# Local attention on one core: the two heads of a pair alternate on halves of TensorE's array (values by columns, scores by rows)

## The chip, the cores and the metric

The kernel runs on one core of a Trainium2 chip. The metric is the device time of one execution in microseconds; the time of a kernel is the median of several runs. TensorE multiplies 128x128 tiles, ScalarE (ACT) and VectorE (DVE) take the results out of PSUM (8 banks of 128 x 512 float32) and prepare operands, GpSimd (POOL) does small things, and SyncE (SP) issues the transfers.

## What is computed

One decoder block on 512 tokens with 1024 features, all in float32: a retention mixer with 4 heads and a sliding-window attention with 8 query heads and 2 key heads run side by side on the same normed input, are gated and merged, and a squared-ReLU MLP follows. The change touches the sliding-window attention only. Of the reference, that is:

```python
SWA_HEADS, SWA_KV_HEADS, SWA_DH, WINDOW = 8, 2, 64, 128
# q: (1, 512, 8, 64); k, v: (1, 512, 2, 64); blocks of 128 tokens
# kk, vv: the previous block and the block itself, 256 keys for each block of queries
s = jnp.einsum('bnigrd,bnjgd->bgrnij', qb, kk).astype(f32) * (dh ** -0.5)
s = s - slopes * dist                       # a slope for each head
s = jnp.where(blk_valid, s, -jnp.inf)       # 0 <= dist < 128; block 0 has no previous block
m = jnp.maximum(jnp.max(s, axis=-1, keepdims=True), sink)
p = jnp.exp(s - m)
p = p / (jnp.sum(p, axis=-1, keepdims=True) + jnp.exp(sink - m))
out = jnp.einsum('bgrnij,bnjgd->bnigrd', p, vv.astype(f32))
```

Around it: `x += RMSNorm((sigmoid(gate_r) * y_r + sigmoid(gate_s) * y_s) @ W_out)`, where `y_s` is this output times `W_swa_out`, and then the MLP.

## The kernel before

Most products are made in three passes of the type float32r: each operand is split into a rounded part (`split`, L124, ACT) and the remainder (L125, DVE), and `mm3` (L167 to L169) multiplies hi by hi, hi by lo and lo by hi. Some small products are made with plain float32 operands instead: the scores of the retention (`ret_scores`, L534), the values of the attention (L506, L510). A plain float32 product leaves two matmul records, and two weight loads, for each call in the trace; a float32r product leaves one.

The attention stage is a loop over 4 steps `h` (L626). Step `h` treats one retention head and one pair of attention heads (2h and 2h+1, which share a key head). In a step TensorE runs, in this order: the scores of the pair (`swa_scores`), the projection of the retention's queries (`project_copy` to `qT`), the transposes of the step before (`ret_out`), the projection of the keys (`kT`), the transposes of the attention's probabilities (`swa_transpose`, L488, L490), those of the keys (`ret_keys`), the next step's retention values (`project_v`), the retention's scores (`ret_scores`), the attention's values (`swa_values`), the retention's states (`ret_states`, tile `ret_st`), two gate projections with the next pair's queries between them (`swa_queries`, L662), and the retention's values (`ret_values`, tile `ret_v`). A planner in the framework sets the order on each engine from the order of the program, priorities and modelled times; `issue_after` holds instructions back behind a named one. All PSUM tiles come from one pool of 8 banks.

Queries of a pair come out of one projection as 128 rows, 64 for each head. `swa_queries` makes for each head `g` a tile `qs2[g]` of 128 rows: the rounded part on the head's own 64 rows (ACT, L419) and the remainder on the other 64 (DVE, L420). The keys `ksT` hold the 64 key rows twice, in a rounded part and a remainder (L623, by `split`). So a score product contracts over 128 rows with a stacked split, and two products (`part`, L446 to L451) over 256 key columns make a block: 16 matmuls of 128x256 for the pair. In step 0 the queries first go through a copy `rg` that multiplies by the norm factors `R` (L389), since that projection is made from the input that is not yet normed.

`swa_values` (L498) multiplies the transposed probabilities with the 64 value columns of the key head. Head 0 writes rows 0 to 63 of one bank `pso`, head 1 rows 64 to 127; all seven products of head 0 come first (one of L506 and one of L510 for each block but block 0), then the seven of head 1. The result is split to `swaT` (L513).

Of the kernel before, what the change touches and what calls it, by code (L numbers as in the profile page):

```python
# [10 lines left out]
F32 = mybir.dt.float32  # L11
F32R = mybir.dt.float32r
AF = mybir.ActivationFunctionType
ALU = mybir.AluOpType
PSUM = bass.MemoryType.PSUM

P = 128
D_MODEL = 1024
SEQ = 512
NT = SEQ // P  # L20
# [67 lines left out]
def f(ap):  # L88
    return ap.bitcast(F32)
# [3 lines left out]
def block_kernel(ctx, tc, x, xT, pre_mix, w_in, w_gate, w_ret, w_swa, w_out, sinks, post_mix,  # L93
# [10 lines left out]
    def bank(shape, name="ps"):  # L104
        return psum.tile(shape, F32, tag="ps", name=name)
# [279 lines left out]
    def project_copy(dst, w, first):  # L385

        ps = project_block(w, xg if first else hT)
        if first:
            nc.vector.tensor_tensor(dst, ps, R, op=ALU.mult)  # L389
        else:  # L390
            nc.scalar.copy(dst, ps)
# [15 lines left out]

    def swa_queries(w, first=False):

        if first:  # L410
            ps = rpool.tile([P, SEQ], F32, name="rg", bufs=2)
            project_copy(ps, w, True)
        else:
            ps = project_block(w)
        rows = [slice(g * SWA_DH, (g + 1) * SWA_DH) for g in range(2)]
        qs2 = []
        for g in range(2):
            q2 = dpool.tile([P, SEQ], F32R, name=f"qs2{g}", bufs=1)
            q_hi = nc.scalar.mul(q2[rows[g]], ps[rows[g]], SWA_DH**-0.5)  # L419
            q_lo = nc.vector.scalar_tensor_tensor(  # L420
                q2[rows[1 - g]], ps[rows[g]], SWA_DH**-0.5, f(q2[rows[g]]),
                op0=ALU.mult, op1=ALU.subtract,
            )
            qs2.append(q2)
        return (qs2, (q_hi, q_lo)) if first else qs2

    def swa_scores(b, qs2):
        bias = dpool.tile([P, 2, 2 * P], F32, name="bias", bufs=1)
        m = asmall.tile([P, 2, NT], F32, name="m")
        den = asmall.tile([P, 2, NT], F32, name="den")  # L430
        sexp = asmall.tile([P, 2, NT], F32, name="sexp")
        negm = asmall.tile([P, 2, NT], F32, name="negm")
        probs = []
        for g in range(2):
            head = 2 * b + g
            nc.vector.tensor_scalar(
                bias[:, g, :], dist_sb, float(2.0 ** (-8.0 / SWA_HEADS * (head + 1))), None,
                op0=ALU.mult,
            )
            s = dpool.tile([P, NT, 2 * P], F32, name="s", tag="s")  # L440
            for bp in range(2):
                ps = bank([P, 2, 2 * P], "swa_s")
                for i in range(2):
                    blk = 2 * bp + i
                    k0 = max(blk - 1, 0) * P
                    for part in range(2):  # L446
                        nc.tensor.matmul(
                            ps[:, i, :], qs2[g][:, blk * P : (blk + 1) * P],
                            ksT[part][:, b // 2, k0 : k0 + 2 * P],
                            start=part == 0, stop=part == 1,  # L450
                        )  # L451
                for i in range(2):
                    blk = 2 * bp + i
                    lo = P if blk == 0 else 0
                    nc.vector.tensor_tensor_reduce(
                        s[:, blk, lo:], ps[:, i, : 2 * P - lo], bias[:, g, lo:], 1.0,
                        sink_sb[:, head : head + 1], ALU.add, ALU.max,
                        accum_out=m[:, g, blk : blk + 1],
                    )
            nc.vector.tensor_scalar(negm[:, g, :], m[:, g, :], -1.0, None, op0=ALU.mult)  # L460
            nc.vector.tensor_scalar(
                sexp[:, g, :], m[:, g, :], -1.0, sink_sb[:, head : head + 1],
                op0=ALU.mult, op1=ALU.add,
            )
            for blk in range(NT):
                lo = P if blk == 0 else 0
                nc.scalar.activation(
                    s[:, blk, lo:], s[:, blk, lo:], AF.Exp, bias=negm[:, g, blk : blk + 1],
                    accum_out=den[:, g, blk : blk + 1],
                )  # L470
            nc.scalar.activation(sexp[:, g, :], sexp[:, g, :], AF.Exp)
            nc.vector.tensor_add(den[:, g, :], den[:, g, :], sexp[:, g, :])
            nc.vector.reciprocal(den[:, g, :], den[:, g, :])
            for blk in range(NT):
                lo = P if blk == 0 else 0
                nc.vector.tensor_scalar(
                    s[:, blk, lo:], s[:, blk, lo:], den[:, g, blk : blk + 1], None, op0=ALU.mult
                )
            probs.append(s)
        return probs  # L480
# [17 lines left out]
    def swa_values(b, probs_t):  # L498
        pso = bank([P, SEQ], "pso")
        c0 = P + (b // 2) * SWA_DH  # L500
        for g, (pd, pp) in enumerate(probs_t):
            rows = slice(g * SWA_DH, (g + 1) * SWA_DH)
            for blk in range(NT):
                o = pso[rows, blk * P : (blk + 1) * P]
                if blk:
                    nc.tensor.matmul(  # L506
                        o, kv[:, blk - 1, c0 : c0 + SWA_DH], pp[:, blk - 1, :],
                        start=True, stop=False,
                    )
                nc.tensor.matmul(  # L510
                    o, kv[:, blk, c0 : c0 + SWA_DH], pd[:, blk, :], start=blk == 0, stop=True
                )
        split(swaT[0][:, b, :], swaT[1][:, b, :], pso)  # L513

# [94 lines left out]

    pending = None  # L610
    q = load_queries(0)
    qs2, qs_last = swa_queries(q[0], True)
    kk2 = dpool.tile([P, SWA_KV, NT, 2, SWA_DH], F32, name="kk2", tag="s")
    ksT = [dpool.tile([P, SWA_KV, SEQ], F32R, name=f"ksT{i}", bufs=1) for i in range(2)]
    for g in range(SWA_KV):
        for i in range(2):
            nc.gpsimd.tensor_copy(kk2[:, g, :, i, :], kv[:, :, g * SWA_DH : (g + 1) * SWA_DH])
        ps = bank([P, SEQ])
        for t in range(NT):
            nc.tensor.transpose(  # L620
                ps[:, t * P : (t + 1) * P], kk2[:, g, t].rearrange("p i d -> p (i d)"), ident
            )
        split(ksT[0][:, g, :], ksT[1][:, g, :], ps)  # L623
    v0_block(3)
    v0_out(3)
    for h in range(RET_HEADS):  # L626
        probs = swa_scores(h, qs2)
        qT = dpool.tile([P, SEQ], F32, name="qT", bufs=1)
        project_copy(qT, q[1], h == 0)
        qc = [dpool.tile([P, SEQ - P], F32R, name=f"qc{i}", bufs=1) for i in range(2)]  # L630
        split(qc[0], qc[1], qT[:, P:])
        if pending is not None:
            ret_out(*pending)
        kr = load_feature_blocks(w_in, (C_KR + h * RET_DK,))
        kT = dpool.tile([P, SEQ], F32, name="kT", bufs=1)
        project_copy(kT, kr[0], h == 0)
        if h == 0:
            with ExitStack() as order:
                for ins in qs_last:
                    order.enter_context(tc.issue_after(ins.ins))  # L640
                for k in range(KD):
                    norm_input(k)
            uctx0.close()
            actx = ExitStack()
            apool = actx.enter_context(tc.tile_pool(name="apool", bufs=1, side="right"))
            retT = [apool.tile([P, KD, SEQ], F32R, name=f"retT{i}") for i in range(2)]
            swaT = [apool.tile([P, 4, SEQ], F32R, name=f"swaT{i}") for i in range(2)]
        probs_t = swa_transpose(probs)
        kd = ret_keys(kT, h)
        v = v_next  # L650
        if h + 1 < RET_HEADS:
            v_next = project_v(h + 1)
        pt = ret_scores(qT, kT, h)
        swa_values(h, probs_t)
        states = ret_states(kd, v, h)
        g = load_feature_pair(w_in, C_GR + h * RET_DV)
        silu = rpool.tile([P, 2, SEQ], F32, name="silu")
        if h + 1 < RET_HEADS:
            q = load_queries(h + 1)
        for e in range(2):  # L660
            if e == QS_AT and h + 1 < RET_HEADS:
                qs2 = swa_queries(q[0])  # L662
            ps = project_block(g[e])
            nc.scalar.activation(silu[:, e, :], ps, AF.Sigmoid)
            nc.vector.tensor_tensor(silu[:, e, :], ps, silu[:, e, :], op=ALU.mult)
        retn = ret_values(qc, pt, states, v, h)
        pending = (retn, silu, h)
# [537 lines left out]
```

## Time and profile before

| | us |
|---|---|
| median of 3 runs | 753.0 (752.38 to 754.23) |
| the profiled execution | 751.75 |
| its span in the profile | 750.0 |
| TensorE busy in the span | 738.2 (98%) |
| VectorE busy | 545.6 (73%) |
| ScalarE busy | 400.1 (53%) |

The profiled execution is 1.75 us longer than its span, and 1.25 us shorter than the median. In the trace a matmul record starts when the array takes it and its end is modelled, so the records of a run of matmuls overlap: the distance from start to start is what one costs. Where a row stands for several instructions (x8), its first number is the first start and its second the time to the last end; the start of the last one is that end less the duration of a single one. PEld is the loading of the stationary operand, which has a row of its own.

### The profile page before, as it was taken

What the parts mean: (1) busy time and instruction counts of PE and PEld (TensorE: products, weight loads), DVE (VectorE), ACT (ScalarE), POOL (GpSimd) and SP (SyncE); (2) the same over time, 40 slices, a digit from 0 to 9 for tenths busy, and PEclk for the clock granted to TensorE, in tenths of its full rate; (3) what the DMA queues carried; (4) which work ended last, traced back from release to release, by engine and by line L of the source; (5) the groups of instructions that cost most, each with busy time, mean ns of one, the idle gap of its engine ahead of it and who ended that gap; (6) DMA issues with size and microseconds to landing.
All of it is one profiled execution on the core that took longest, in us unless ns stands there. A gap on an engine that the chain in (4) does not pass through costs nothing.

```text
span 750.0 us, 11710 instructions
## 1 busy us (share of the span) xinstructions
PE 738.2 (98%) x4678; PEld 668.5 (89%) x4678; DVE 545.6 (73%) x847; ACT 400.1 (53%) x642; POOL 50.1 (7%) x67
## 2 busy tenths in 40 slices
PE   8999999999999999999999999999999999999996
PEld 8979899898888989899888999999999888888885
DVE  5695474655868867776755787688779778986796
ACT  6683464354554544343542775566556655655571
POOL 0200000000001000000001200000000011010010
PEclk9999999999999999999999999999999999999999
DMA  8614312312015584553483326876763899789503
GB/s 298 202 56 142 97 44 59 111 29 85 29 57 155 144 241 122 141 146 100 147 324 113 94 62 218 205 195 170 185 169 113 292 296 206 173 180 214 112 1 112
DMA packets 51863, 109.42 MB, mean 146 GB/s; under 512 B 3425, under 2 KB 31457, under 8 KB 47713
## 3 DMA queue, kind: packets, MB, share of 16 engines
q1 hardware_dynamic: 46480, 80.89, 32.3%
q0 software_dynamic: 5328, 27.79, 20.1%
q8 instruction: 36, 0.59, 0.3%
q14 instruction: 19, 0.15, 0.1%
HBM read 106.57 MB, written 2.10 MB: 145 GB/s over the span
## 4 chain that ended last, share of the span: by engine, by line
PE 81%; DVE 8%; DMA 7%; issue 2%; ACT 1%; SPq 0%; POOL 0%; POOLq 0%; DVEq 0%; ACTq 0%
PE wino L169 8%; PE wino L167 8%; PE wino L168 8%; PE p L167 5%; PE p L169 5%; PE p L168 5%; PE pblk L167 5%; PE pblk L169 5%; PE pblk L168 5%; DVE wlo L125 2%; PE yr L169 2%; PE yr L167 2%; PE yr L168 2%; PE ps L167 2%; PE ps L168 2%; PE ps L169 2%
## 5 line engine op out<-in xcount | busy, mean ns | idle before, releaser
L125 DVE TENSOR_TENSOR wlo<-raw,whi 128x1024 fp32r<-128x1024 f32 x89 | 108.4, 1221 | 73.5 <-ACT whi L124 73.4
L124 ACT CAST whi<-raw 128x1024 fp32r<-128x1024 f32 x89 | 93.2, 1051 | 108.4 <-PE pblk L168 35.4
L167 PE MATMUL p<-whi,left 128*128 128x512 f32 x216 | 84.0, 390 | 0.1
L168 PE MATMUL p<-wlo,left 128*128 128x512 f32 x216 | 84.1, 389 | 0.0
L169 PE MATMUL p<-whi,left 128*128 128x512 f32 x216 | 84.0, 390 | 0.0
L167 PE MATMUL pblk<-hT,whi 128*128 128x512 f32 x136 | 53.3, 392 | 0.0
L168 PE MATMUL pblk<-hT,whi 128*128 128x512 f32 x136 | 53.0, 390 | 0.0
L169 PE MATMUL pblk<-hT,wlo 128*128 128x512 f32 x136 | 52.9, 389 | 0.0
L169 PEld LDWEIGHTS p<-whi,left 128*128 128x128 f32 x216 | 40.6, 188 | 8.7 <-DVE left L125 0.4
L167 PEld LDWEIGHTS p<-whi,left 128*128 128x128 f32 x216 | 40.5, 188 | 8.8 <-ACT left L124 0.5
L168 PEld LDWEIGHTS p<-wlo,left 128*128 128x128 f32 x216 | 40.6, 188 | 8.6
L125 DVE TENSOR_TENSOR left<-uc,left 128x1024 fp32r<-128x1024 f32 x28 | 34.1, 1222 | 14.9 <-ACT left L124 14.9
L124 ACT CAST left<-uc 128x1024 fp32r<-128x1024 f32 x28 | 29.3, 1048 | 25.5 <-PE p L168 24.1
L125 DVE TENSOR_TENSOR wlo<-tch,whi 128x1024 fp32r<-128x1024 f32 x32 | 38.8, 1219 | 2.8 <-ACT whi L124 2.8
L124 ACT CAST whi<-tch 128x1024 fp32r<-128x1024 f32 x32 | 33.4, 1047 | 10.8 <-PE p L169 8.4
L124 ACT CAST whi<-rs 128x1024 fp32r<-128x1024 f32 x21 | 22.0, 1049 | 31.4 <-PE wino L168 12.6
L125 DVE TENSOR_TENSOR wlo<-rs,whi 128x1024 fp32r<-128x1024 f32 x21 | 25.6, 1219 | 10.8 <-ACT whi L124 10.8
L970 ACT ACTIVATE uc<-uc 128x512 f32<-128x512 f32 x26 | 15.0, 624 | 29.8 <-DVE uc L256 29.8
L169 PEld LDWEIGHTS pblk<-hT,wlo 128*128 128x128 f32 x136 | 25.5, 188 | 5.4
L167 PEld LDWEIGHTS pblk<-hT,whi 128*128 128x128 f32 x136 | 25.6, 188 | 5.0
L168 PEld LDWEIGHTS pblk<-hT,whi 128*128 128x128 f32 x136 | 25.6, 188 | 5.0
L169 PE MATMUL wino<-h2s,p 128*128 128x256 f32 x104 | 29.5, 284 | 0.4 <-DVE p L125 0.4
(328 smaller groups left out, 2347.5 us busy)
## 6 DMA issues: line engine op xcount, KB each, us to landing
tch<-in_w_down POOLq DMA_DIRECT2D x12, 1024.0 KB, 8.4
raw<-in_w_in SPq DMA_DIRECT2D x14, 512.0 KB, 5.6
raw<-in_w_in SPq DMA_DIRECT2D x7, 1024.0 KB, 5.5
raw<-in_w_down SPq DMA_DIRECT2D x7, 1024.0 KB, 7.4
rs<-in_w_up SPq DMA_DIRECT2D x13, 512.0 KB, 4.2
rs<-in_w_up POOLq DMA_DIRECT2D x13, 512.0 KB, 6.9
raw<-in_w_up SPq DMA_DIRECT2D x13, 512.0 KB, 5.2
raw<-in_w_gate SPq DMA_DIRECT2D x8, 512.0 KB, 4.2
```

Source lines behind the costliest of these rows:

```text
L124: nc.scalar.copy(hi, src)
L125: last["split"] = nc.vector.tensor_tensor(lo, src, f(hi), op=ALU.subtract)
L167: nc.tensor.matmul(ps, ah, bh, start=first, stop=False)
L168: nc.tensor.matmul(ps, ah, bl, start=False, stop=False)
L169: nc.tensor.matmul(ps, al, bh, start=False, stop=last)
L970: nc.scalar.activation(rb, rb, AF.Relu, scale=(1.0, -1.0)[b])
```

## The change

`swa_queries` keeps one tile `qs` in plain float32, head 0 on rows 0 to 63 and head 1 on rows 64 to 127, written by one instruction: on ACT in steps 1 to 3, and in step 0 by a DVE instruction that multiplies by the scale and by `R` at once, straight from PSUM. The keys `ksT` become one float32 tile, copied by ACT; its two copies of the 64 key rows stay. `swa_scores` takes its four banks at the start and makes one float32 product of 64 contracted rows for each head and block, the two heads in turn, each in banks of its own; block 0 has 128 key columns in place of 256. The bias, the maxima, the exponentials and the rest of `swa_scores` are as before. `swa_values` makes the same products as before in another order: by block, the two heads in turn. In step 0 the normed input (`norm_input`) is now held back behind the one instruction that writes `qs`.

```diff
--- before.py
+++ after.py
@@ -407,29 +407,34 @@
 
     def swa_queries(w, first=False):
 
+        qs = dpool.tile([P, SEQ], F32, name="qs", bufs=1)
+        ps = project_block(w, xg if first else hT)
         if first:
-            ps = rpool.tile([P, SEQ], F32, name="rg", bufs=2)
-            project_copy(ps, w, True)
+            last["qs"] = nc.vector.scalar_tensor_tensor(
+                qs, ps, SWA_DH**-0.5, R, op0=ALU.mult, op1=ALU.mult
+            )
         else:
-            ps = project_block(w)
-        rows = [slice(g * SWA_DH, (g + 1) * SWA_DH) for g in range(2)]
-        qs2 = []
-        for g in range(2):
-            q2 = dpool.tile([P, SEQ], F32R, name=f"qs2{g}", bufs=1)
-            q_hi = nc.scalar.mul(q2[rows[g]], ps[rows[g]], SWA_DH**-0.5)
-            q_lo = nc.vector.scalar_tensor_tensor(
-                q2[rows[1 - g]], ps[rows[g]], SWA_DH**-0.5, f(q2[rows[g]]),
-                op0=ALU.mult, op1=ALU.subtract,
-            )
-            qs2.append(q2)
-        return (qs2, (q_hi, q_lo)) if first else qs2
-
-    def swa_scores(b, qs2):
+            nc.scalar.mul(qs, ps, SWA_DH**-0.5)
+        return qs
+
+    def swa_scores(b, qs):
         bias = dpool.tile([P, 2, 2 * P], F32, name="bias", bufs=1)
         m = asmall.tile([P, 2, NT], F32, name="m")
         den = asmall.tile([P, 2, NT], F32, name="den")
         sexp = asmall.tile([P, 2, NT], F32, name="sexp")
         negm = asmall.tile([P, 2, NT], F32, name="negm")
+
+        banks = [[bank([P, 2, 2 * P], "swa_s") for _ in range(2)] for _ in range(2)]
+        for blk in range(NT):
+            k0 = max(blk - 1, 0) * P
+            k1 = (blk + 1) * P
+            for g in range(2):
+                rows = slice(g * SWA_DH, (g + 1) * SWA_DH)
+                nc.tensor.matmul(
+                    banks[blk // 2][g][:, blk % 2, : k1 - k0],
+                    qs[rows, blk * P : (blk + 1) * P], ksT[rows, b // 2, k0:k1],
+                    start=True, stop=True,
+                )
         probs = []
         for g in range(2):
             head = 2 * b + g
@@ -439,16 +444,7 @@
             )
             s = dpool.tile([P, NT, 2 * P], F32, name="s", tag="s")
             for bp in range(2):
-                ps = bank([P, 2, 2 * P], "swa_s")
-                for i in range(2):
-                    blk = 2 * bp + i
-                    k0 = max(blk - 1, 0) * P
-                    for part in range(2):
-                        nc.tensor.matmul(
-                            ps[:, i, :], qs2[g][:, blk * P : (blk + 1) * P],
-                            ksT[part][:, b // 2, k0 : k0 + 2 * P],
-                            start=part == 0, stop=part == 1,
-                        )
+                ps = banks[bp][g]
                 for i in range(2):
                     blk = 2 * bp + i
                     lo = P if blk == 0 else 0
@@ -498,17 +494,20 @@
     def swa_values(b, probs_t):
         pso = bank([P, SEQ], "pso")
         c0 = P + (b // 2) * SWA_DH
-        for g, (pd, pp) in enumerate(probs_t):
-            rows = slice(g * SWA_DH, (g + 1) * SWA_DH)
-            for blk in range(NT):
-                o = pso[rows, blk * P : (blk + 1) * P]
-                if blk:
+
+        o = [pso[g * SWA_DH : (g + 1) * SWA_DH] for g in range(2)]
+        for blk in range(NT):
+            sl = slice(blk * P, (blk + 1) * P)
+            if blk:
+                for g in range(2):
                     nc.tensor.matmul(
-                        o, kv[:, blk - 1, c0 : c0 + SWA_DH], pp[:, blk - 1, :],
-                        start=True, stop=False,
+                        o[g][:, sl], kv[:, blk - 1, c0 : c0 + SWA_DH],
+                        probs_t[g][1][:, blk - 1, :], start=True, stop=False,
                     )
+            for g in range(2):
                 nc.tensor.matmul(
-                    o, kv[:, blk, c0 : c0 + SWA_DH], pd[:, blk, :], start=blk == 0, stop=True
+                    o[g][:, sl], kv[:, blk, c0 : c0 + SWA_DH], probs_t[g][0][:, blk, :],
+                    start=blk == 0, stop=True,
                 )
         split(swaT[0][:, b, :], swaT[1][:, b, :], pso)
 
@@ -609,9 +608,9 @@
 
     pending = None
     q = load_queries(0)
-    qs2, qs_last = swa_queries(q[0], True)
+    qs = swa_queries(q[0], True)
     kk2 = dpool.tile([P, SWA_KV, NT, 2, SWA_DH], F32, name="kk2", tag="s")
-    ksT = [dpool.tile([P, SWA_KV, SEQ], F32R, name=f"ksT{i}", bufs=1) for i in range(2)]
+    ksT = dpool.tile([P, SWA_KV, SEQ], F32, name="ksT", bufs=1)
     for g in range(SWA_KV):
         for i in range(2):
             nc.gpsimd.tensor_copy(kk2[:, g, :, i, :], kv[:, :, g * SWA_DH : (g + 1) * SWA_DH])
@@ -620,11 +619,11 @@
             nc.tensor.transpose(
                 ps[:, t * P : (t + 1) * P], kk2[:, g, t].rearrange("p i d -> p (i d)"), ident
             )
-        split(ksT[0][:, g, :], ksT[1][:, g, :], ps)
+        nc.scalar.copy(ksT[:, g, :], ps)
     v0_block(3)
     v0_out(3)
     for h in range(RET_HEADS):
-        probs = swa_scores(h, qs2)
+        probs = swa_scores(h, qs)
         qT = dpool.tile([P, SEQ], F32, name="qT", bufs=1)
         project_copy(qT, q[1], h == 0)
         qc = [dpool.tile([P, SEQ - P], F32R, name=f"qc{i}", bufs=1) for i in range(2)]
@@ -635,9 +634,7 @@
         kT = dpool.tile([P, SEQ], F32, name="kT", bufs=1)
         project_copy(kT, kr[0], h == 0)
         if h == 0:
-            with ExitStack() as order:
-                for ins in qs_last:
-                    order.enter_context(tc.issue_after(ins.ins))
+            with tc.issue_after(last["qs"].ins):
                 for k in range(KD):
                     norm_input(k)
             uctx0.close()
@@ -659,7 +656,7 @@
             q = load_queries(h + 1)
         for e in range(2):
             if e == QS_AT and h + 1 < RET_HEADS:
-                qs2 = swa_queries(q[0])
+                qs = swa_queries(q[0])
             ps = project_block(g[e])
             nc.scalar.activation(silu[:, e, :], ps, AF.Sigmoid)
             nc.vector.tensor_tensor(silu[:, e, :], ps, silu[:, e, :], op=ALU.mult)
```

## Rows read from the trace of the kernel before

**Rows 1.** The page: busy time, share of the span and instructions of each engine.
```profile
PE 738.2 (98%) x4678; PEld 668.5 (89%) x4678; DVE 545.6 (73%) x847; ACT 400.1 (53%) x642; POOL 50.1 (7%) x67
```
**Rows 2.** Waits of TensorE, whole span: who for whom, total us, times, longest.
```profile
PE swa_s L447 <- DVE ksT L125: 0.9, 1, 0.9
PE yr L169 <- DVE wlo L125: 0.5, 1, 0.5
```
**Rows 3.** Busy time by stretch (step 0, step 1): us, PE, PEld, DVE, ACT, POOL, clock.
```profile
28.00:67.00 39.00, 38.04 (x249) 34.05 (x247) 32.35 (x74) 23.11 (x52) 1.69 (x4) 1.00 0.33 95
...
92.00:130.00 38.00, 38.00 (x250) 34.35 (x250) 23.56 (x64) 19.35 (x45) 1.02 (x1) 1.00 0.23 65
```
**Rows 4.** Timeline of TensorE, step 1, values: start us, us, line, tile, count.
```profile
117.11 1.06 PE L534 MATMUL ret_s<-qT,kT 128*128 128x128 f32 x8
118.10 0.43 PE L510 MATMUL pso<-pd,kv 128*64 128x128 f32 x2
...
119.24 0.27 PE L506 MATMUL pso<-pp,kv 128*64 128x128 f32 x1
119.25 0.32 PE L510 MATMUL pso<-pd,kv 128*64 128x128 f32 x1
...
119.41 0.33 PE L510 MATMUL pso<-pd,kv 128*64 128x128 f32 x2
...
119.74 0.38 PE L510 MATMUL pso<-pd,kv 128*64 128x128 f32 x2
...
120.61 0.38 PE L510 MATMUL pso<-pd,kv 128*64 128x128 f32 x2
120.92 0.39 PE L167 MATMUL ret_st<-v,kd 128*128 128x256 f32 x1
121.14 0.28 PE L168 MATMUL ret_st<-v,kd 128*128 128x256 f32 x1
121.26 0.28 PE L169 MATMUL ret_st<-v,kd 128*128 128x256 f32 x1
```
**Rows 5.** Timeline of weight loads (PEld), step 0, where head 1's values begin.
```profile
68.21 0.25 PEld L506 LDWEIGHTS pso<-pp,kv 128*64 128x64 f32 x2
68.32 0.24 PEld L510 LDWEIGHTS pso<-pd,kv 128*64 128x64 f32 x3
```
**Rows 6.** Timeline of TensorE, step 1, around the scores.
```profile
90.02 2.08 PE L447 MATMUL swa_s<-ksT,qs 128*128 128x256 f32 x16
91.94 0.40 PE L167 MATMUL pblk<-hT,whi 128*128 128x512 f32 x1
```
**Rows 7.** Timeline of step 0, TensorE, DVE and ACT around the first scores.
```profile
35.16 0.58 ACT L124 CAST ksT<-ps 128x512 fp32r<-128x512 f32 x1
35.52 0.68 DVE L389 TENSOR_TENSOR rg<-pblk,R 128x512 f32<-128x512 f32 x1
36.23 1.28 ACT L419 ACTIVATE qs<-rg 64x512 fp32r<-64x512 f32 x2 [0.50 <-DVE rg L389]
37.37 1.40 DVE L420 SCALAR_TENSOR_TENSOR qs<-rg,qs 64x512 fp32r<-64x512 f32 x2
38.11 0.51 PE L447 MATMUL swa_s<-ksT,qs 128*128 128x256 f32 x2
38.80 1.29 DVE L125 TENSOR_TENSOR ksT<-ps,ksT 128x512 fp32r<-128x512 f32 x2
39.55 1.94 PE L447 MATMUL swa_s<-ksT,qs 128*128 128x256 f32 x14 [0.94 <-DVE ksT L125]
41.33 0.40 PE L167 MATMUL pblk<-xg,whi 128*128 128x512 f32 x1
```
**Rows 8.** Timeline of DVE, step 0: what follows the projection of the keys.
```profile
52.73 0.69 DVE L389 TENSOR_TENSOR kT<-pblk,R 128x512 f32<-128x512 f32 x1 [0.93 <-PE pblk L169]
```
**Rows 9.** Timeline of step 1, DVE and TensorE: retention's norm and its transposes.
```profile
94.06 1.90 DVE L590 TENSOR_SCALAR retn<-ret_v,mv,rr 128x256 f32<-128x256 f32 x4 [0.74 <-POOL rr L588]
97.41 1.03 PE L600 MATMUL ret_t<-ident,retn 128*128 128x128 f32 x8
```

## The prediction, made before the changed kernel was run

> **What bounds the kernel now.** I read the shares of busy time first: TensorE is busy 98% of the span, VectorE 73%, ScalarE 53% [rows 1]. Then the waits of TensorE: two show, 0.9 us before the first scores, on the split of the keys, and 0.5 us much later [rows 2]. Then the stretches: in step 1 TensorE is busy all 38.00 us and VectorE 23.56; in step 0 TensorE loses about 1 us of 39 [rows 3]. So in steps 1 to 3 only what shortens TensorE's own row shortens the kernel; work taken from ACT or DVE there is worth nothing by itself. In step 0 the wait counts too. Behind the attention TensorE stays the bound, with waits that hang on work which moves along with it, so a microsecond won in the loop should arrive at the end. "Busy" does not mean that the array is full: what a matmul costs is the distance from its start to the next, so I work with starts from here on.
>
> **Values.** The pair's 14 calls leave 28 records. Head 0's first ten records stand 0.11 us apart (118.10 to 119.24, 1.14 us), head 1's at the end likewise (119.74 to 120.61 is 8 records, 0.87 us, 0.109 each) [rows 4]. In between, head 1's first record starts at 119.25, 0.01 us behind one of head 0, while three more of head 0 are still to come: from 119.24 to 119.74 there are eight starts in 0.50 us, 0.0625 each [rows 4]. The two heads write different column halves, and there they run side by side, at full rate each. The pattern stands at the same place in all four steps, of which one is shown. The change makes it the rule for all 28.
>
> Going into this mode and out of it costs something, before and after alike. The scores of the retention, 8 records from 117.11, have their last start near 117.90 (117.11 + 1.06 - 0.27), 0.11 apart; the values begin 0.20 later, 0.09 too late, and the first gap in them adds 0.05. On the way out the last start is 120.72, the states start at 120.92, 0.09 too late, and their second at 121.14, 0.22 where 0.12 is normal (121.14 to 121.26) [rows 4]. Together 0.33 us. The stretch from 118.01, where a next record of the old mode was due, to 121.02, where the states are back in their rhythm, is 3.01 us. After the change it is 14 x 0.109 = 1.53 at best, or 28 x 0.0625 = 1.75 if the rate of the overlapped eight is a limit, plus 0.33: 1.86 to 2.08, so 0.93 to 1.15 us less. I take the middle, 1.03, in each step: **4.1 us**. Nothing else moves: the casts of `pso` come after the last product in both kernels.
>
> [...] The rows show that weight loads of head 1 (three of L510 from 68.32) start inside the time of head 0's products [rows 5], and that products of both heads then start in turn [rows 4]. [...]
>
> **Scores.** Before, 16 records run from 90.02 to 91.94, 1.92 us [rows 6]. After, each head has 128 + 3 x 256 = 896 key columns, seven units of 128, in two records each. The nearest row for a plain float32 product of that width in weights is the retention's scores, 0.11 us for a record of 128 columns [rows 4]; taking the time as proportional to the columns, a head needs 7 x 2 x 0.11 = 1.55 us, and a pair 1.55 side by side or 3.10 one after the other. No row of the trace shows two row halves. The bounds are these two, and the nearest row to decide between them is the overlap of the column halves [rows 4], so I take side by side. To this comes a new entry and exit, which the old scores, in the same mode as their neighbours, did not pay: 0 to 0.33, and I take 0.33 from the values. And 16 weight loads of 128 columns might share one path: no record with weights of that width starts closer than 0.11 to the next, so 16 x 0.11 = 1.76 would replace 1.55. The ends for side by side are 1.55 and 2.09; I take 2.0. In steps 1 to 3 that is 0.08 us more each, **-0.25 us**.
>
> [...] What the rows show is the 0.33 us around the values [rows 4]. [...]
>
> **Step 0.** Here the scores occupy TensorE from 38.05 to 41.33, 3.28 us, since the first two start behind the second remainder of the queries (DVE, 37.37 + 1.40) and the others at 39.55 behind the remainders of the keys (DVE, 38.80 + 1.29) [rows 7]. After the change one DVE instruction like L389 (0.68 from 35.52) ends at about 36.2 and `qs` is ready; 2.69 us of DVE work and the two ACT instructions of 1.28 us are gone [rows 7], so ACT's second copy of the keys, which stood behind those, can follow the first (35.16 + 0.58) and end by 36.4. Both are ready before TensorE is through with the work ahead of the scores at about 38. So the stretch becomes 2.0: **+1.3 us** (1.2 to 1.7). What is late next? TensorE's two projections follow from 41.33 without waiting. Behind them DVE waits 0.93 us for TensorE before it takes `kT` at 52.73 [rows 8], and DVE itself has 2.69 us less to do, so its chain moves up with TensorE. If some weight cast did not move up, up to 1.3 us would be lost again.
>
> **The rest at nothing.** In steps 1 to 3 DVE loses two instructions and ACT has one in place of two; TensorE waits for neither [rows 2, 3], so 0. The maxima of head 0's third and fourth block now wait for the end of all scores. Queued behind them on DVE is the retention's norm (94.06 to 95.96), and its reader on TensorE starts at 97.41 [rows 9]: 1.45 us of cover, and the scores end within 0.1 us of where they did. No DMA is moved or added, and the same four banks are taken.
>
> **Sum.** 4.1 - 0.25 + 1.3 = 5.15 us. The profiled execution of 751.75 would become 746.6; the median of the runs stands 1.25 above it, so **747.85 us**, 0.7% less. The ends of this case: best, 4 x 1.15 + 3 x 0.37 + 1.73 = 7.4 us, 745.6; worst, 4 x 0.93 - 3 x 0.17 + 0 = 3.2 us, 749.8.
>
> **The rivals.**
>
> Row halves in turn, column halves together. For it: no row shows row halves, and each half of the rows fills all 128 output rows, while the two heads' values write different ones. Against: the column halves overlap without being asked to. The scores take 3.10 + 0.33 = 3.43: -0.15 in step 0, -1.51 in the others. 4.1 - 0.15 - 4.53 = -0.6 us, 753.6 us: no difference.
>
> [...]
>
> Slower: row halves in turn, and each change of half is an entry of its own. Its price is the 0.09 + 0.05 us of the entry into the values [rows 4], at the 7 changes of head between the 8 calls: 1.0 us a pair. The scores take 3.43 + 1.0 = 4.43 us: 4.1 - 1.15 - 7.5 = -4.55, 757.55 us. It decides from 3.85 us for a pair's scores, that is from 0.06 us a change; below, the time is within 0.3%.
>
> [...]
>
> **How the numbers follow.** About 0.3%, 2.3 us, is what a measurement of this kernel can tell from no change. Forecast 0.74, its own range 745.6 to 749.8; row halves in turn 0.12, 753.6; column halves in turn or another order 0.08, 752; slower 0.06, 757.55. The forecast's range holds 0.74 at most, so the range has to reach to the first two rivals: 745.6 to 753.8. Faster 0.76 (the forecast, and the best of the second rival), same 0.17, slower 0.07.
>
> **What would show it.** Values: records of the two heads in turn, the states starting about 2.0 us after the retention's scores end, in place of 3.0. Scores: 16 records of 64 rows in about 2.0 us; starts of the two heads 0.0 to 0.1 apart mean side by side, 0.22 apart in strict turn mean the first rival. Step 0: no wait before the scores, their stretch 2.0 us, and the keys' projection 1.3 us earlier with no new wait behind it. The prediction is wrong if the scores need over 3 us, if the values keep 0.109 between all starts, or if a wait of over 1 us appears behind step 0.

## The result and the profile after

The changed kernel takes 748.62 us (median of 6 runs, 747.32 to 749.89), the kernel before 752.44 in the runs beside it (6 runs, 751.50 to 754.23): a ratio of 0.9944, 95% interval 0.9928 to 0.9961, 4.2 us less. In a later session the same pair gave 747.86 and 754.03, a ratio of 0.9919 (0.9904 to 0.9935). The two intervals share only 0.9928 to 0.9935; the changed kernel's medians agree within 0.8 us and it is the kernel before that differs by 1.6 us. Part of it goes with the granted TensorE clock: of the kernel before's 29 runs in the session of the first experiments, the ten with a mean clock of 0.998 or more have a median of 752.7 us, the nine with 0.995 or less 754.2, with 759.8 the longest. The rest stays open. 747.85 us was forecast, 5.15 below the median then known.

The profiled execution of the changed kernel has a span of 745.5 us where the kernel before had 750.0. Where the 4.5 us arose is read from the time at which TensorE reaches the same place in both (starts in us, from the timelines of TensorE):

| | before | after | earlier by |
|---|---|---|---|
| step 0, scores begin | 38.11 | 38.11 | 0.00 |
| step 0, transposes of the probabilities | 52.53 | 51.13 | 1.40 |
| step 0, values begin | 67.18 | 67.08 | 0.10 |
| step 0, states begin | 70.00 | 68.76 | 1.24 |
| step 1, scores begin | 90.02 | 88.88 | 1.14 |
| step 1, values begin | 118.10 | 116.96 | 1.14 |
| step 1, states begin | 120.92 | 118.64 | 2.28 |
| step 2, states begin | 171.86 | 168.52 | 3.34 |
| step 3, states begin | 211.29 | 207.03 | 4.26 |

Every gain that lasts falls between the beginning of the values and that of the states: 1.14, 1.14, 1.14 and 1.00 us. The scores change nothing in step 1 (1.14 when they begin, 1.14 when its values do), nor in steps 2 and 3, and what step 0's scores gained is gone before its values begin. Behind the attention both kernels run alike: 538.71 us are left in the one and 538.47 in the other.

TensorE's waits name the place in step 0. The wait for the keys' split [rows 2] is gone, and a new one stands second, the longest in the loop (waits of TensorE, whole span, after: total us, times, longest):

```profile
PE warm L297 <- POOL ident masks.py:199: 1.4, 1, 1.4
PE ret_k L520 <- DVE kT L389: 1.1, 1, 1.1
PE ptok L167 <- ACT xg L301: 1.0, 1, 1.0
```

The values of step 1 after, where [rows 4] show them before (timeline of TensorE: start, us to the last end, line, tile, count):

```profile
115.97 1.06 PE L533 MATMUL ret_s<-qT,kT 128*128 128x128 f32 x8
116.96 0.44 PE L508 MATMUL pso<-pd,kv 128*64 128x128 f32 x4
117.23 0.39 PE L503 MATMUL pso<-pp,kv 128*64 128x128 f32 x4
117.45 0.39 PE L508 MATMUL pso<-pd,kv 128*64 128x128 f32 x4
...
118.32 0.39 PE L508 MATMUL pso<-pd,kv 128*64 128x128 f32 x4
118.64 0.38 PE L167 MATMUL ret_st<-v,kd 128*128 128x256 f32 x1
```

Four records now start every 0.22 us where two did, 28 in 1.68 us (116.96 to 118.64) in place of 2.82 (118.10 to 120.92). The way in is as before, the last score near 116.76 and the first value 0.20 later.

The scores of step 1 after, where [rows 6] show them before, with a neighbour on either side:

```profile
88.67 0.28 PE L169 MATMUL ret_v<-st,qc 128*128 128x256 f32 x1
88.88 1.79 PE L433 MATMUL swa_s<-ksT,qs 64*128 64x128 f32 x16
90.59 0.50 PE L167 MATMUL pblk<-hT,whi 128*128 128x512 f32 x1
90.93 0.39 PE L168 MATMUL pblk<-hT,whi 128*128 128x512 f32 x1
91.16 0.39 PE L169 MATMUL pblk<-hT,wlo 128*128 128x512 f32 x1
```

The tile of the array reads 64*128 now. The 16 records take 1.71 us to the next product in place of 1.92. But the first comes 0.21 behind its neighbour where 0.12 is the rhythm there, and the second product behind them 0.34 behind the first where 0.23 is: 0.20 us more outside the 1.71, so 1.91 in place of 1.92. That the two heads run side by side is read from the records counted from the beginning of the scores on (busy time of TensorE in a stretch, those of `swa_s` alone: stretch, us, busy with the number of records, clock, DMA):

```profile
88.87:88.89 0.02, 0.01 (x2) 1.00 0.00 0
88.87:89.08 0.21, 0.20 (x2) 1.00 0.00 0
88.87:89.10 0.23, 0.23 (x4) 1.00 0.00 0
```

Two records start within 0.02 us, none for the next 0.19, then again two. In the trace all eight pairs stand so, their two starts less than 0.01 apart.

Step 0 on DVE, after (timeline of DVE), where [rows 8] stand before:

```profile
50.23 1.19 DVE L125 TENSOR_TENSOR wlo<-raw,whi 128x1024 fp32r<-128x1024 f32 x1
51.34 1.07 DVE L472 TENSOR_SCALAR s<-s,den 128x128 f32<-128x128 f32 x4
52.33 1.22 DVE L125 TENSOR_TENSOR wlo<-raw,whi 128x1024 fp32r<-128x1024 f32 x1
53.46 0.68 DVE L389 TENSOR_TENSOR kT<-pblk,R 128x512 f32<-128x512 f32 x1
```

and on TensorE:

```profile
51.13 0.60 PE L484 MATMUL psd<-ident,s 128*128 128x128 f32 x4
51.56 0.49 PE L486 MATMUL psp<-ident,s 128*128 128x128 f32 x3
51.89 0.91 PE L484 MATMUL psd<-ident,s 128*128 128x128 f32 x4
52.63 0.49 PE L486 MATMUL psp<-ident,s 128*128 128x128 f32 x3
54.20 0.55 PE L520 MATMUL ret_k<-ident,kT 128*128 128x128 f32 x3 [1.08 <-DVE kT L389]
54.51 0.36 PE L167 MATMUL ptok<-whi,hT 128*128 128x256 f32 x1
```

The projection of the keys is over at about 51.1, but DVE takes `kT` out of PSUM at 53.46 only. A weight split of 1.2 us (52.33) stands between the last probabilities and `kT`. In the order of DVE's instructions it is the first half of the gates' weights, `g[0]` of L656 in the kernel before, which TensorE reads from 69.93 on. Before, the copy of `kT` came first [rows 8], and the four splits that stand here at 46.82, 50.23, 52.33 and 54.06 all followed it (timeline of DVE, before):

```profile
54.00 2.35 DVE L125 TENSOR_TENSOR wlo<-raw,whi 128x1024 fp32r<-128x1024 f32 x2
...
56.80 2.35 DVE L125 TENSOR_TENSOR wlo<-raw,whi 128x1024 fp32r<-128x1024 f32 x2
```

So TensorE waits 1.08 us; from start to start the transposes of the keys come 1.24 late (52.63 to 54.20, where 0.33 is the rhythm). The second group of `psd` (0.91 where the first took 0.60) has lost 0.3 before that.

### The profile page after: what moved, and what is told of

Its sections match the earlier page's. It is cut to its first block, busy times and chain, and to the rows that moved or that the text cites. A ratio compares the mean times of both kernels' runs of the same rounds, so it can differ in the third digit from the quotient of the medians.

```text
span 745.5 us, 11695 instructions
## 1 busy us (share of the span) xinstructions
PE 733.3 (98%) x4678; PEld 661.6 (89%) x4678; DVE 538.0 (72%) x837; ACT 397.1 (53%) x637; POOL 50.4 (7%) x67
## 4 chain that ended last, share of the span: by engine, by line
PE 79%; DVE 9%; DMA 8%; ACT 2%; issue 2%; SPq 0%; POOL 0%; POOLq 0%; DVEq 0%; ACTq 0%
PE wino L169 8%; PE wino L167 8%; PE wino L168 8%; PE p L167 5%; PE p L169 5%; PE p L168 5%; PE pblk L167 4%; PE pblk L168 4%; PE pblk L169 4%; DVE wlo L125 2%; PE yr L169 2%; PE yr L168 2%; PE yr L167 2%; PE ps L167 2%; PE ps L169 2%; PE ps L168 2%
```

## The experiments

Theory A: the values carry the gain, since column halves run side by side wherever the two heads are close enough in the queue; the scores break even; step 0's gain is real but is lost to DVE's order. Theory B: the scores and the relief of DVE and ACT carry a good part of it.

**The values alone.** The kernel before with the new `swa_values`; all else as before.

```diff
-        for g, (pd, pp) in enumerate(probs_t):
-            rows = slice(g * SWA_DH, (g + 1) * SWA_DH)
-            for blk in range(NT):
...
+        for blk in range(NT):
+            if blk:
+                for g in range(2):
...
+            for g in range(2):
```

> The kernel before with the new order of the values alone; scores, queries and keys as before. Theory A (the values carry the gain): the stretch from the end of the retention's scores to the states falls from 3.0 to 1.9 us in each of the four steps, 4.5 us in all; span 750.0 - 4.5 = 745.5, as much as the whole change. Theory B (half of the gain or more comes from the scores and from the work taken off DVE and ACT): span 747.5 or more.

748.96 us (12 runs) against 753.94 for the kernel before: ratio 0.9937 (0.9914 to 0.9960). Its profiled execution has a span of 749.4, which taken alone is what theory B asks for. But its scores began 0.47 later, and behind the attention it lost 3.5 us (542.2 left, where the kernel before has 538.7): TensorE waited 2.0 us for a weight split in the MLP (0.4 in the kernel before), and the granted clock was 0.50 in the 2 us just behind that wait (stretch, us, busy time of TensorE with the number of records, clock, DMA):

```profile
480.00:482.00 2.00, 2.00 (x11) 0.50 0.94 250
```

None of this touches the values. From the first scores to the last states it is 168.60 us, against 173.18 in the kernel before: 4.58 less. The places say the same: from the values to the states 1.67, 1.69, 1.69 and 1.68 us in the four steps. In step 1:

```profile
117.42 0.44 PE L512 MATMUL pso<-pd,kv 128*64 128x128 f32 x4
...
119.11 0.38 PE L167 MATMUL ret_st<-v,kd 128*128 128x256 f32 x1
```

That is 4 times 1.14 less. With the ratio it bears out A: the new order of the values gives by itself about what the whole change gives.

**The scores alone.** The changed kernel with `swa_values` as before.

> The changed kernel with the values in their old order, head after head. Theory A: the scores end 1.5 us earlier in step 0 but 1.1 us of it stay in a wait of TensorE for the copy of the retention's keys on DVE, and the scores of steps 1 to 3 cost what they did; span 749.5 to 750. Theory B: span 747.5 or less.

752.36 us (12 runs) against 753.94: ratio 0.9983 (0.9969 to 0.9997), 1.6 us less by the medians and 1.3 by the ratio, and a span of 750.4, 0.4 over theory A's range. The sign is just clear of no change. In the trace the wait stands as in the changed kernel:

```profile
54.01 0.55 PE L517 MATMUL ret_k<-ident,kT 128*128 128x128 f32 x3 [1.08 <-DVE kT L389]
```

and from the beginning of the first scores to that of the values it is 29.39 us, where the kernel before has 29.07; to the last states it is 173.76, where that has 173.18. B falls. A holds for the place of the loss. That the medians show 1.3 to 1.6 us and these places of the trace none is left open; the kernel before's one trace has a span of 750.0, where its 29 runs beside these experiments have a median of 752.2, while 750.4 is near this kernel's own median of 750.6.

**Row halves in turn.** The changed kernel with the scores head after head.

```diff
-        for blk in range(NT):
-            k0 = max(blk - 1, 0) * P
-            k1 = (blk + 1) * P
-            for g in range(2):
+        for g in range(2):
+            for blk in range(NT):
+                k0 = max(blk - 1, 0) * P
+                k1 = (blk + 1) * P
```

> The changed kernel with its scores head after head: four products on the upper row half, then four on the lower. If row halves overlap only where both have products close ahead in the queue, as the old values did (head 1 began while four records of head 0 were left), a pair's scores take about 2.5 us in place of 1.9: 0.6 us in each of steps 1 to 3, step 0 hidden in its wait; span 747.3. If the order doesn't matter, because the engine finds the other half's products wherever they stand: 745.5. If row halves never run side by side and the 1.9 us have another reason: 745.5 too, with starts in strict turn.

751.24 us (10 runs), ratio 0.9963 (0.9948 to 0.9978), against 748.62 and a ratio of 0.9944 for the changed kernel. In step 1:

```profile
90.84 2.55 PE L433 MATMUL swa_s<-ksT,qs 64*128 64x128 f32 x16
93.32 0.51 PE L167 MATMUL pblk<-hT,whi 128*128 128x512 f32 x1
```

2.48 us to the next product in place of 1.71: 0.77 more a pair, three times, 2.3 us. Wholly in turn it would have been some 3.1 by the prediction's estimate; side by side throughout it is 1.7. So row halves do run side by side, also with plain float32, and only as far as the other head's products are near: the first outcome of the three. In step 1 the records counted from the beginning are

```profile
90.84:91.59 0.75, 0.75 (x4) 1.00 0.00 0
90.84:91.62 0.78, 0.78 (x6) 1.00 0.02 4
```

so the fifth and the sixth start together, at 91.60 and 91.61 in the trace: the lower half begins when four of the upper half's eight are left, as with the values, though all but the first two of a head have 256 columns here (in the changed kernel's trace a pair of these takes 0.22 us to the next where a pair of 128 columns takes 0.11). Its span of 750.3 also holds a start 1.45 us later than in the changed kernel's profile; the scores' own row is what counts here.

**The keys first.** The changed kernel with another order of DVE in step 0: the copy in `project_copy` is remembered, and the bias products of step 1 and the splits of step 0's gate weights are queued behind it. The load itself is issued as before.

```diff
+            last["kT"] = nc.vector.tensor_tensor(dst, ps, R, op=ALU.mult)
...
+            with tc.issue_after(last["kT"].ins) if b == 1 else ExitStack():
...
-        g = load_feature_pair(w_in, C_GR + h * RET_DV)
+        if h == 0:
...
+            with tc.issue_after(last["kT"].ins):
+                g = [parts(raw[:, :, b * P : (b + 1) * P], [P, KD, P]) for b in range(2)]
```

> The changed kernel, with one change of order in step 0: on DVE the weight splits for the gates and the two bias products of step 1 are queued behind the copy of the retention's keys (kT). Theory A (the gain of step 0 is lost to DVE's order: the copy stands behind a weight split of 1.1 us that nobody needs yet): the wait of 1.1 us before the transposes of the keys goes, span 744.4, ratio to the kernel before about 0.9925. Rival (DVE is full there in any order, and what is put behind the copy is missed later): the wait moves to the next weights or values, span 745.5.

746.36 us (6 runs), ratio 0.9907 (0.9883 to 0.9930), span 744.0. The waits of TensorE, whole span, have lost the one for `kT` and none has come in its place:

```profile
PE warm L297 <- POOL ident masks.py:199: 1.4, 1, 1.4
PE ptok L167 <- ACT xg L301: 1.0, 1, 1.0
PE yr L169 <- DVE wlo L125: 0.5, 1, 0.5
```

On DVE `kT` now stands in front of both splits:

```profile
51.16 1.07 DVE L473 TENSOR_SCALAR s<-s,den 128x128 f32<-128x128 f32 x4
52.14 0.68 DVE L389 TENSOR_TENSOR kT<-pblk,R 128x512 f32<-128x512 f32 x1
52.74 2.35 DVE L125 TENSOR_TENSOR wlo<-raw,whi 128x1024 fp32r<-128x1024 f32 x2
```

From the first scores to the values it is 27.50 us, against 28.97 in the changed kernel and 29.07 before. The gain of step 0, 1.5 us, arrives at last. The rival, a DVE that is full in any order, falls: the 0.71 and 2.46 us for which DVE waits soon after (at 56.73 and 59.61) were room enough.

**Side by side once more.** The changed kernel and the one with the keys first, on one chip.

> The changed kernel once more, for a comparison beside the next run on the same chip: ratio to the kernel before 0.994.

> The same order of DVE in step 0 as in the run with the keys first, beside the changed kernel on one chip. If the wait for kT (1.1 us) and the 0.3 us before it are all that the order cost, this is 1.3 to 1.5 us below the changed kernel; if the 2 us that separate their ratios in different sessions are real, something else moved too.

747.86 and 746.41 us (6 runs each) against 754.03 for the kernel before: ratios 0.9919 (0.9904 to 0.9935) and 0.9903 (0.9886 to 0.9921). 1.45 us between the medians, as expected from the wait and the 0.3 before it. From the first scores to the values the two traces have 29.38 and 27.38, 2.00 apart: in this trace of the changed kernel the transposes lose 0.7 before the same wait, where the earlier one lost 0.3, so that part differs from run to run. The intervals overlap, so the medians alone would not settle it; the wait does, which stands in all traces of the changed order and in neither with the keys first. Of all kernels run, the one with the keys first is the fastest.

**Values in longer runs.** The changed kernel; each head treats two blocks before the other has its turn.

```diff
-        for blk in range(NT):
-            sl = slice(blk * P, (blk + 1) * P)
+        for half in range(2):
+            for g in range(2):
+                for blk in (2 * half, 2 * half + 1):
+                    sl = slice(blk * P, (blk + 1) * P)
```

> The changed kernel with the values in longer runs: blocks 0 and 1 of head 0, the same of head 1, then blocks 2 and 3 of each: runs of 6, 6, 8 and 8 records. If at most five records of the two heads can be on their way at once (in the old order head 1 began when four of head 0 were left), 18 record times of 0.109 are needed in place of 14: the stretch from the end of the retention's scores to the states grows from 1.9 to 2.3 us, 0.4 us in each step, span 1.7 us over the changed kernel. If the order only has to name both heads within the 28 records, it stays at 1.9; if no overlap outlasts a change of head by more than it did in the old order, 2.5 us or more.

748.78 us (4 runs), ratio 0.9932 (0.9914 to 0.9949), 0.9 above the changed kernel in the same session, whose runs lie up to 2.4 us apart. In step 1:

```profile
117.53 0.43 PE L508 MATMUL pso<-pd,kv 128*64 128x128 f32 x2
117.80 0.27 PE L504 MATMUL pso<-pp,kv 128*64 128x128 f32 x1
117.81 0.32 PE L508 MATMUL pso<-pd,kv 128*64 128x128 f32 x1
...
119.39 0.38 PE L508 MATMUL pso<-pd,kv 128*64 128x128 f32 x2
119.70 0.38 PE L167 MATMUL ret_st<-v,kd 128*128 128x256 f32 x1
```

From values to states 2.17 us in each of the four steps, between the 1.68 of turns by call (1.82 in step 3) and the 2.82 of the old order, 0.49 over the first. The count with five records on their way gave 0.44. Three times 0.49 and 0.35 in step 3 are 1.8 us, of which the medians show 0.9 and the spans (746.7 and 746.0) 0.7. In the two traces the rest is given back elsewhere: 0.6 between the scores and the values of step 0 (28.76 in place of 29.38) and 0.4 behind the attention, places that this edit doesn't touch and that differ from run to run. Here too head 1 begins at 117.81, 0.01 behind head 0's third record and with three more of head 0 still to come, as in the old order it began behind the eleventh of 14 [rows 4]. In these runs the beginning goes with the count of records left, four each time, and not with the place in the run. Four records are two calls; no run tells which of the two is counted.

## Why the prediction was right, and where it was not

- **TensorE's row bounds the steps 1 to 3, and a gain there arrives at the end.** Right: 4.26 us at the last states, 4.5 at the end.
- **The values, 4.1 us.** Right in mechanism, a little small in size. The stretch of the prediction, from where a next score was due (116.87) to where the states are back in rhythm (118.74), is 1.87 us where 1.86 was the best end and 1.97 the middle taken. So the rate of 0.0625 that I feared from the eight overlapped starts was no limit: 28 records at 0.0545 fit, and the 0.33 us for going in and out stayed. Three steps gave 1.14, step 3 gave 1.00 (1.82 us in place of 1.68; why is open), together 4.4.
- **Column halves in turn, or another order (the second rival: 0.08, 752).** It fell. That alternated values keep their time, on which these 752 us rest, no run shows. In the trace of the changed kernel the products of both heads' values fill 128 rows and 64 columns of the array (128*64), the heads stand in turn as the program has them, and the values take 1.67 to 1.82 us in all four steps, alone (first experiment) as within the change, in place of 2.82.
- **The scores, -0.25 us.** Side by side was right. The size was off by 0.09 a step: 1.91 us in place of 2.0, because of 16 weight loads that I thought might share one path; without an allowance for them the prediction's own 1.55 + 0.33 gives 1.88. They start 0.08 apart on the average (1.39 us for 16, the last taking 0.19), closer than the 0.11 I took as their bound, and in the trace they too stand in pairs, less than 0.01 apart:

```profile
38.11 1.39 PEld L433 LDWEIGHTS swa_s<-ksT,qs 64*128 64x128 f32 x16
```

- **Going in and out of the mode.** Found once a step. Counted as the 0.33 around the values was, the scores lose 0.09 us before their first record, 0.10 in the first gap (the second pair starts 0.21 behind the first, where a record of 128 columns takes 0.11), 0.09 before the next product and 0.11 before its second: 0.4, a little more than the 0.33. It eats what row halves would have gained: 1.71 + 0.20 against 1.92. That it is paid once a step and not at each change of head was an estimate of mine, which no row of before showed for row halves; the trace of the changed kernel shows 0.4 us at the ends, and less than 0.01 from one head's start to the other's.
- **Step 0, 1.3 us.** This step failed. The prediction had named a new wait of over 1 us as a sign of being wrong, and 1.08 us is what came. The scores did as forecast: no wait before them, 1.72 us (38.11 to 39.83) in place of 3.22 (the prediction's 3.28 counts from 38.05, where no score starts). ACT's copies of the keys ended at 38.14, not by 36.4; that cost nothing here and 0.30 us in the second trace of this kernel. The sentence that failed is "its chain moves up with TensorE". I had taken DVE's idle 0.93 us before `kT` [rows 8] for slack, and the order behind it as given. The order is made anew with each program: in the new one three of the four weight splits that had come after `kT` stand before it, the last of them right in front, and `kT` was copied 0.73 us later (53.46) than before (52.73) although TensorE delivered it 1.4 us sooner. The loss of up to 1.3 us by a weight cast was named, as one that does not move up; what happened is a cast that moved up too far. The experiment with the keys first shows it by giving the time back. Why the planner moved the splits, for the 2.69 us of work taken off DVE or for the other edits of step 0, no run separates.
- **The sum.** 5.15 forecast; 4.4 + 0.0 + 0.1 = 4.5 in the trace, 4.2 in the runs beside it. The shortfall of step 0 (1.2) was partly covered by what the values (+0.3) and the scores (+0.25) did better than their terms. That the total came close is in part luck, such a balance.
- **The rivals.** Row halves in turn and column halves in turn both fell by the timelines. The slower one, a stall at each change of head, fell with them: 16 records in 1.71 us, in pairs less than 0.01 apart, leave no room for seven stalls.

## What to carry to other kernels

Products that fill only half of the array's rows or columns went faster here when the two halves took turns call by call: 28 records of the values in 1.68 us where head after head took 2.82, 16 of the scores in 1.71 where head after head took 2.48. Look in the trace for a place where two halves meet by chance, since it shows whether they overlap. Count the way into and out of such a mode, 0.33 to 0.4 us a stretch here, against the gain: 14 short products in 28 records repaid it well, scores that were already packed by another means did not. When a change takes work off an engine whose order a planner makes, read the new order before counting on the gain: what is freed may be filled with work that is not yet needed, in front of work that is.

## What the runs showed of the hardware

- Plain float32 products on the two row halves, and on the two column halves, run side by side at nearly full rate: 28 records of 128 columns in 1.68 us, where records of one half stand 0.109 apart, and 16 records of 64 rows in 1.71, where head after head took 2.48. The starts of the two halves mostly stand less than 0.01 apart; in the values of step 3 it is 0.03.
- The other half began when four records of a run were left, in runs of 14 and 6 with column halves and in a run of 8 with row halves. The values cost 2.17 us in runs of 6 to 8 records, where turns of 2 cost 1.68 and runs of 14 cost 2.82.
- Weight loads of 128 columns for two row halves started 0.08 us apart on the average (16 in step 0 of the changed kernel), in pairs less than 0.01 apart.
- The granted clock was 0.50 in the stretch from 480 to 482 us, just behind a wait of TensorE of 2.0 us, in the run with the values alone. The mean clock of that execution was 0.995, of the kernel before's profiled one 0.998.
